# Moving a float32 decoder trunk's up-projections and mixer outputs to tokens on the partitions, with block transposes on VectorE and small transfers inside SBUF

## The chip, the cores and the metric

The kernel runs on one core of a Trainium2 chip. A core has a matrix engine (TensorE; PE in the profile, PEld for its weight loads), a vector engine (VectorE, DVE), a scalar engine (ScalarE, ACT), a general engine (GpSimd, POOL) and a queue engine (SyncE, SP). Each runs its own instructions in order and waits on semaphores for the others. Transfers are issued by SP, ACT or POOL and carried out by 16 DMA engines. SBUF is the on-chip memory of 128 partitions, PSUM the accumulators that TensorE writes. The metric is device time in microseconds (us) of one launch.

## The reference, cut to what matters

A residual stream `x` of 256 tokens by 2048 features goes through two layers, all in float32.

```python
h = rms_norm(x, mix_norm[l])
h = mixer_ab(h, ...)              # layer 0: gMLP (8 heads) beside HGRN2 (8 heads), then @ ab_w_out
h = mixer_c(h, ...)               # layer 1: forgetting attention, 16 heads, then @ c_w_out
x = x + h
h = rms_norm(x, ffn_norm[l])
z = h @ w_up                      # 2048 -> 2 * 5632
z = conv_w[0]*z[t-2] + conv_w[1]*z[t-1] + conv_w[2]*z[t] + conv_b    # per feature, along the tokens
a, b = split(z, 2)
x = x + (silu(a) * b) @ w_down    # 5632 -> 2048
```

The convolution runs along the tokens, so it wants a feature's tokens side by side in one partition.

## The kernel before, in words

**Products.** Every float32 operand of a large product is held as two rounded parts, high and low, and a product is three: high by high, low by high, high by low. `weights` (lines 130 to 142) loads a chunk of weights on SP, ScalarE makes the high part `wh` (line 139), VectorE the low part `wl` (line 141). `split` (199 to 206) does the same for activations; a tile of 512 columns holds 256 tokens of high part and then 256 of low part. A block below means 128 inputs by 128 outputs of a weight, over all 256 tokens.

There are two forms of a product. In `project` (144 to 161) the weights are the operand that TensorE holds and the activations stream past: per block one matmul of 512 columns with `wh` (line 155) and one of 256 columns with `wl` (line 158), and the output has features on the partitions. In `project_tok` (163 to 184) and in `down` (line 727 to 729) 128 tokens of activations are held and 512 output features stream past: three matmuls of 512 columns for each half of the tokens and each 128 inputs, and the output has tokens on the partitions. Four blocks then take six matmuls.

**Stages.** `mixer_ab` uses `project_tok` for v and i, `project` for f, q, g and u, and `project` for the output `w_abo`: 16 outputs of 16 blocks, each added to the stream `xT` by `add_x` (263) and handed to the next norm by `feed`, which splits it and adds its square to a running sum. `ffn` then runs `up` and `down`. `up` makes 11 hidden tiles at a time: `conv` (658) calls `project_norm`, that is a product in the first form, `fold` (ScalarE copies one half out of PSUM, VectorE adds the other), a multiplication by the norm's `R`, and the convolution (667 to 669) on ScalarE and VectorE; then silu, product and split. `down` accumulates each group of 11 in the token form into `y`; at the last group `turn` (688) transposes `y` on TensorE (line 692, 64 transposes in the program), except for the last quarter of the outputs, which uses `project` and `add_x`. `mixer_c` has q, k and v in token form, the gate in `project`, and its output `w_co` in `project` as `w_abo`. The number of blocks in the first form is 2816 in the two up-projections, 256 in each mixer output, 88 in `down` and 784 elsewhere: 4200.

**What sets the order.** The program is traced in Python and a scheduler orders each engine's instructions by when they could start, taking the traced order first among those that could. Work that may lie beside products is written as generators in `queue`; `tick`, called at each chunk of weights, advances at most `depth` of them by a step. `weights` draws from a pool `wp` with 4 buffers of `w` and 3 each of `wh` and `wl`; in the MLPs every other chunk uses a second pool (`deep`) with 4 and 2. PSUM has four banks for products (`pm`). At the start 15 matmuls on ones (WARM) run before the first product; the table FETCH sets when pieces of `x` are loaded, most of them on SP.

Of the kernel before, what the change touches and what calls it, by code (L numbers as in the profile page):

```python
# [14 lines left out]
P = 128  # L15
S = 256
# [6 lines left out]
GRP = 11  # L23
EPS = 1e-6
WARM = 15
FETCH = {0: (0,), 1: (1, 2, 8), 2: (4, 6), 3: (12,)}
# [19 lines left out]
def tile_trunk(ctx: ExitStack, tc: tile.TileContext, x, pp_d, cst_d, mlev_d, msk_d,  # L46
# [24 lines left out]
    pp = cp.tile([P, NPP], F32, tag="pp", name="pp")  # L71
    cst = cp.tile([P, NK], F32, tag="cst", name="cst")
    ones = cp.tile([P, P], F32, tag="ones", name="ones")
    one1 = cp.tile([P, 1], F32, tag="one1", name="one1")

    nc.sync.dma_start(pp[:, 0:C_FFN], pp_d[:, 0:C_FFN])
# [23 lines left out]
    def back(ap):  # L100
        return view(ap, P - 1, (-1, P))

# [27 lines left out]
    def weights(src, n, rows=None):  # L130
        deep["turn"] += 1
        if deep["pool"] is not None and deep["turn"] > 6 and deep["turn"] % 2:
            pool, nw, ns = deep["pool"], 4, 2
        else:
            pool, nw, ns = wp, 4, 3
        w = pool.tile([P, n], F32, tag="w", name=nm("w"), bufs=nw)
        nc.sync.dma_start(w if rows is None else w.rearrange("p (m c) -> p m c", m=rows), src)
        wh = pool.tile([P, n], F32R, tag="wh", name=nm("wh"), bufs=ns)
        SC.activation(wh, w, AF.Copy)  # L139
        wl = pool.tile([P, n], F32R, tag="wl", name=nm("wl"), bufs=ns)  # L140
        V.tensor_tensor(wl, w, wh.bitcast(F32), ALU.subtract)  # L141
        return wh, wl

    def project(wsrc, acts, chunks=(8, 8), k0=0, run=2):
        ps = pm.tile([P, 512], F32, tag="pm", name=nm("pm"))
        nk = sum(chunks)
        done = 0
        for c in chunks:
            lo = (k0 + done) * P
            tick()  # L150
            wh, wl = weights(wsrc[:, lo:lo + c * P], c * P)
            for k1 in range(0, c, run):
                ks = range(k1, min(k1 + run, c))
                for k in ks:
                    PE.matmul(ps, wh[:, k * P:(k + 1) * P], acts[done + k],  # L155
                              start=done + k == 0, stop=False, skip_group_check=True)
                for k in ks:
                    PE.matmul(ps[:, S:2 * S], wl[:, k * P:(k + 1) * P], acts[done + k][:, 0:S],  # L158
                              start=False, stop=done + k == nk - 1, skip_group_check=True)
            done += c  # L160
        return ps

    def project_tok(wsrc, norm, feed=False):
        ps = [pm.tile([P, 512], F32, tag="pm", name=nm("pm")) for _ in range(2)]
        k = 0
        for c in ((1, 1, 1, 1) + (2,) * 6 if feed else (2,) * 8):
            if feed:
                for c0 in FETCH.get(k, ()):
                    t, c0, n = fetch[c0]
                    (SC if c0 >= 8 else nc.sync).dma_start(t, x[:, c0:c0 + n, :])  # L170
                for i in range(c):
                    norm.feed_split(k + i)
            tick()
            wh, wl = weights(wsrc[:, k * 512:(k + c) * 512], c * 512)
# [9 lines left out]
        return ps  # L184

# [13 lines left out]
    def split(dst, src, gain=None):  # L199
        if gain is None:  # L200
            SC.activation(dst[:, 0:S], src, AF.Copy)
            V.tensor_tensor(dst[:, S:2 * S], src, dst[:, 0:S].bitcast(F32), ALU.subtract)
        else:
            SC.activation(dst[:, 0:S], src, AF.Copy, scale=gain)
# [3 lines left out]
    def rsq(dst, src, n):  # L208
        tag = "sq" if dst.shape[-1] == S else f"rm{len(dst.shape)}{dst.shape[-1]}"
        m = tp.tile(list(dst.shape), F32, tag=tag, name=nm("rm"))  # L210
        t = tp.tile(list(dst.shape), F32, tag=tag, name=nm("rt"))
# [11 lines left out]
    class Norm:  # L223
        def __init__(self, col):
            self.col = col
            self.a = [None] * KT
            self.acc = cp.tile([P, S], F32, tag="acc", name=nm("acc"), bufs=2)
            self.n = 0

        def feed_split(self, k):  # L230
            a = apool.tile([P, 512], F32R, tag="a", name=nm("a"), bufs=KT)
            split(a, xT[k], pp[:, self.col + k:self.col + k + 1])
            self.a[k] = a
# [13 lines left out]

        def finish(self, tok=False):
# [6 lines left out]
            p2 = bank()  # L255
            for T in range(2):
                PE.matmul(p2[:, 2 * T:2 * T + 2], self.acc[:, T * P:(T + 1) * P], ones[:, 0:2],
                          start=True, stop=True)
            Rt = cp.tile([P, 2], F32, tag="Rt", name=nm("Rt"), bufs=2)
            rsq(Rt, p2[:, 0:4].rearrange("p (t two) -> p t two", two=2)[:, :, 0], D)  # L260
            return R, Rt

    def add_x(m, ps):
# [3 lines left out]
        V.tensor_tensor(xT[m], xT[m], t, ALU.add)  # L267


    def mixer_ab(norm):  # L270
# [90 lines left out]
        ge = hp.tile([P, 3 * NH], F32, tag="ge", name="ge")  # L361
# [32 lines left out]
        def hgrn(h):  # L394
# [15 lines left out]
            for li in reversed(range(NL)):  # L410
# [8 lines left out]
                if li:  # L419
                    V.tensor_tensor(odd, odd, view(tot, m, (-m, 2), (2, m // 2), (0, n)), ALU.mult)  # L420
                    nt = hp.tile([P, m], F32, tag=f"tot{n}", name=nm("tot"), bufs=1)
# [34 lines left out]
            so = hp.tile([P, 2], F32, tag="so", name=nm("so"), bufs=2)  # L456
# [33 lines left out]
        def gated(b):  # L490
# [3 lines left out]
            split(yB[8 + b], lf[b])  # L494
            yield

        def spatial(b, z):
# [3 lines left out]
            split(yB[b], z)  # L501
# [20 lines left out]
        nxt = Norm(C_FFN)  # L522
        ks = [yB[8 + h] for h in range(NH)] + [yB[h] for h in range(NH)]
        for m in range(KT):
            add_x(m, project(w_abo[m], ks, run=2))
            nxt.feed(m)
# [4 lines left out]
    def mixer_c(norm):  # L531
# [4 lines left out]
        R, Rt = norm.finish(tok=True)  # L536
# [4 lines left out]
        gq = hp.tile([P, 1], F32, tag="gq", name="gq")  # L541
# [23 lines left out]
        def attend(h, q, k, v):  # L565
# [20 lines left out]
            mxs = hp.tile([P, 2], F32, tag="mxs", name=nm("mxs"), bufs=2)  # L586
            sms = hp.tile([P, 2], F32, tag="sms", name=nm("sms"), bufs=2)
# [22 lines left out]
        for g in range(CH // 4):  # L610
            qkv = []
            ss = hp.tile([P, 2, 2, 4], F32, tag="ss", name=nm("ss"), bufs=2)
            for j in range(3):
                ps = project_tok(w_cqkv[j * (CH // 4) + g], norm)
# [15 lines left out]
        for h in range(CH):  # L630
# [5 lines left out]
            for b, z in todo:  # L636
# [3 lines left out]
                split(yB[b], z)  # L640
            todo = []
        nxt = Norm(C_FFN + KT)
        for m in range(KT):
            add_x(m, project(w_co[m], yB, run=2))
            nxt.feed(m)
# [4 lines left out]
    def ffn(l, norm, last):  # L650
# [4 lines left out]
        R = norm.finish()  # L655
        nxt = None if last else Norm(C_MIX + KT)

        def conv(j):
            z = project_norm(w_up[l, j], A, R, run=2)

            def w(i):
# [4 lines left out]
            c = hp.tile([P, S], F32, tag="conv", name=nm("conv"), bufs=4)  # L666
# [5 lines left out]
        def up(g):  # L672
            hid = []
            for i in range(GRP):
                j = g * GRP + i
                a = conv(j)
                b = conv(HT + j)
                act(a, a, AF.Silu)
                V.tensor_tensor(a, a, b, ALU.mult)
                t = hp.tile([P, 512], F32R, tag="hid", name=nm("hid"), bufs=2 * GRP)  # L680
                split(t, a)
                hid.append(t)
            return hid
# [4 lines left out]
        def turn(m0):  # L688
            for m in range(m0, m0 + 4, 2):
                tps = bank()  # L690
                for i in range(4):
                    PE.transpose(tps[:, i * P:(i + 1) * P],  # L692
                                 y[:, i % 2, (m + i // 2) * P:(m + i // 2 + 1) * P], ident)
                for i in range(2):
                    V.tensor_tensor(xT[m + i], xT[m + i], tps[:, i * S:(i + 1) * S], ALU.add)
# [7 lines left out]
        def down(g, hid):  # L703
            final = g == HT // GRP - 1
            late = []
            for q in range(4):
                if final and q == 3:
                    for m in range(4 * q, KT):
                        ps = project(w_dn[l, m], hid, chunks=(6, 5), k0=g * GRP, run=2)
                        if late:  # L710
                            late.pop()()
                            turn(4 * q)
                        add_x(m, ps)
                        finish_x(m)
                    return
                ps = [pm.tile([P, 512], F32, tag="pm", name=nm("pm")) for _ in range(2)]
                for k in range(0, GRP, 2):
                    c = min(2, GRP - k)
                    lo = (g * GRP + k) * P
                    wh, wl = weights(w_dn[l, 4 * q:4 * q + 4, :, lo:lo + c * P]  # L720
                                     .rearrange("m p c -> p m c"), 4 * c * P, 4)
                    for T in range(2):
                        for i in range(c):
                            a = hid[k + i]
                            ah, al = a[:, T * P:(T + 1) * P], a[:, S + T * P:S + (T + 1) * P]
                            h, lo_ = (view(t, i * P, (c * P, 4), (1, P)) for t in (wh, wl))
                            PE.matmul(ps[T], ah, h, start=k + i == 0, stop=False)  # L727
                            PE.matmul(ps[T], ah, lo_, start=False, stop=False)  # L728
                            PE.matmul(ps[T], al, h, start=False, stop=k + i == GRP - 1)  # L729
                    if k == 4 and late:  # L730
                        late.pop()()
                for T in range(2):
                    d = y[:, T, q * 512:(q + 1) * 512]
                    if g == 0:
# [3 lines left out]
                if final:  # L738
                    def done(m0=4 * q):
                        turn(m0)  # L740
                        for m in range(m0, m0 + 4):
                            finish_x(m)
                    late.append(done)

        hids = [up(0)]
        for g in range(HT // GRP):
            if g + 1 < HT // GRP:
                hids.append(up(g + 1))
            down(g, hids[g])
# [88 lines left out]
```

## Time and profile before

Three runs took 2359.57, 2360.89 and 2361.82 us. The profiled execution took 2359.05 us, 1.85 us more than its span; the median is 1.84 us above it.

| | us | share of the span | instructions |
|---|---|---|---|
| span of the profiled execution | 2357.2 | | 33532 |
| PE | 2348.7 | 100% | 12528 |
| PEld | 2011.1 | 85% | 12528 |
| DVE | 1689.0 | 72% | 2760 |
| ACT | 1286.3 | 55% | 2085 |
| POOL | 0.2 | 0% | 4 |
| 16 DMA engines, SP's queue | | 55.3% | 193424 packets, 434.20 MB |

The granted TensorE clock was 1.000 throughout. A busy share is time in which the engine had an instruction in flight; matmuls overlap each other, so the rate of PE is read from the distance of their starts. In a group's line, "a | b, c | d" stands for shapes and count, busy us and mean ns of one, and idle us of the engine before them with what ended it. In the timeline a row is one or several instructions of a line: start, length, engine, line, operation, operands.

### The profile page before, as it was taken

Reading aid. Unit: us, or ns where it says so; the run is one execution under the profiler, and the core shown is the slowest. Engines: PE = TensorE matmul, PEld = TensorE weight load, DVE = VectorE, ACT = ScalarE, POOL = GpSimd, SP = SyncE. Lnnn points to the kernel's source line nnn. Section 1 sums busy time; section 2 is a strip of 40 time slices with the busy share of each in tenths; the row PEclk is TensorE's granted clock in tenths of the full one; section 3 lists DMA queues with packets and bytes.
Section 4 is the critical chain, followed back from the end, with each engine's and each line's share of the span. In section 5 each row is a group of like instructions: output and inputs, shape, how many; then the busy total and the mean of one; then the engine's idle time right before and its main releaser. Section 6 shows DMA issues by size and latency. Waiting matters only on the chain.

```text
span 2357.2 us, 33532 instructions
## 1 busy us (share of the span) xinstructions
PE 2348.7 (100%) x12528; PEld 2011.1 (85%) x12528; DVE 1689.0 (72%) x2760; ACT 1286.3 (55%) x2085; POOL 0.2 (0%) x4
## 2 busy tenths in 40 slices
PE   9999999999999999999999999999999999999999
PEld 7888888888888888888888888888888888888887
DVE  7777877878847757866766666777878757758755
ACT  7655665655545545544555455556555545545533
POOL 0000000000000000000000000000000000000000
PEclk9999999999999999999999999999999999999999
DMA  7544455655555565555655554556555565565563
GB/s 269 179 166 150 150 197 206 222 188 188 179 196 196 184 192 197 184 181 164 202 171 180 171 161 169 188 188 239 190 190 189 179 203 190 179 202 191 178 193 117
DMA packets 194740, 439.56 MB, mean 186 GB/s; under 512 B 14208, under 2 KB 108688, under 8 KB 194448
## 3 DMA queue, kind: packets, MB, share of 16 engines
q1 hardware_dynamic: 193424, 434.20, 55.3%
q10 hardware_dynamic: 1152, 3.21, 0.4%
q8 instruction: 98, 1.61, 0.3%
q14 instruction: 66, 0.54, 0.1%
HBM read 435.24 MB, written 2.11 MB: 186 GB/s over the span
## 4 chain that ended last, share of the span: by engine, by line
PE 99%; DMA 0%; ACT 0%; DVE 0%; SPq 0%; issue 0%; ACTq 0%
PE pm L155 42%; PE pm L158 21%; PE pm L728 6%; PE pm L727 6%; PE pm L729 6%; PE pm L181 5%; PE pm L182 5%; PE pm L180 5%; PE px L432 1%; DMA w<-in_w_v 0%; PE px L606 0%; PE px L692 0%; PE px L570 0%; PE px L577 0%; PE px L601 0%; PE px L402 0%
## 5 line engine op out<-in xcount | busy, mean ns | idle before, releaser
L141 DVE TENSOR_TENSOR wl<-w,wh 128x1024 fp32r<-128x1024 f32 (+1 forms) x840 | 1004.3, 1196 | 556.2 <-ACT wh L139 553.9
L139 ACT ACTIVATE wh<-w 128x1024 fp32r<-128x1024 f32 (+1 forms) x840 | 871.1, 1038 | 962.2 <-PE pm L155 473.1
L155 PE MATMUL pm<-a,wh 128*128 128x512 f32 x3600 | 1135.3, 396 | 0.0
L158 PEld LDWEIGHTS pm<-a,wl 128*128 128x128 f32 x3600 | 676.1, 188 | 158.9
L158 PE MATMUL pm<-a,wl 128*128 128x256 f32 x3600 | 708.7, 278 | 0.0
L155 PEld LDWEIGHTS pm<-a,wh 128*128 128x128 f32 x3600 | 549.6, 189 | 1.5 <-DVE a L205 0.8
L727 PE MATMUL pm<-wh,hid 128*128 128x512 f32 x660 | 257.1, 390 | 0.0
L728 PE MATMUL pm<-wl,hid 128*128 128x512 f32 x660 | 256.8, 389 | 0.0
L729 PE MATMUL pm<-wh,hid 128*128 128x512 f32 x660 | 256.8, 389 | 0.0
L180 PE MATMUL pm<-wh,a 128*128 128x512 f32 x512 | 203.1, 398 | 2.6 <-ACT wh L139 2.6
L181 PE MATMUL pm<-wl,a 128*128 128x512 f32 x512 | 200.8, 392 | 0.6 <-DVE wl L141 0.6
L182 PE MATMUL pm<-wh,a 128*128 128x512 f32 x512 | 200.2, 391 | 0.0
L729 PEld LDWEIGHTS pm<-wh,hid 128*128 128x128 f32 x660 | 123.9, 188 | 25.7
L727 PEld LDWEIGHTS pm<-wh,hid 128*128 128x128 f32 x660 | 123.9, 188 | 25.5
L728 PEld LDWEIGHTS pm<-wl,hid 128*128 128x128 f32 x660 | 123.9, 188 | 25.3
L180 PEld LDWEIGHTS pm<-wh,a 128*128 128x128 f32 x512 | 96.2, 188 | 22.4 <-ACT wh L139 3.7
L181 PEld LDWEIGHTS pm<-wl,a 128*128 128x128 f32 x512 | 96.2, 188 | 21.3 <-DVE wl L141 2.2
L182 PEld LDWEIGHTS pm<-wh,a 128*128 128x128 f32 x512 | 96.1, 188 | 19.8
L667 ACT ACTIVATE conv<-ev,pp 128x256 f32<-128x256 f32 x176 | 102.9, 585 | 5.5 <-DVE ev L196 5.5
L189 DVE TENSOR_TENSOR ev<-pm,ev 128x256 f32<-128x256 f32 x225 | 93.9, 417 | 1.1 <-ACT ev L188 1.0
L669 DVE SCALAR_TENSOR_TENSOR conv<-ev,pp,conv 128x254 f32<-128x254 f32 x176 | 85.0, 483 | 6.2
L668 DVE SCALAR_TENSOR_TENSOR conv<-ev,pp,conv 128x255 f32<-128x255 f32 x176 | 84.1, 478 | 4.4 <-ACT conv L667 4.4
(185 smaller groups left out, 1644.3 us busy)
## 6 DMA issues: line engine op xcount, KB each, us to landing
w<-in_w_up SPq DMA_DIRECT2D x352, 512.0 KB, 4.2
w<-in_w_dn SPq DMA_DIRECT2D x150, 512.0 KB, 3.6
w<-in_w_cqkv SPq DMA_DIRECT2D x96, 512.0 KB, 3.5
w<-in_w_abo SPq DMA_DIRECT2D x32, 512.0 KB, 3.6
w<-in_w_cg SPq DMA_DIRECT2D x32, 512.0 KB, 3.6
w<-in_w_co SPq DMA_DIRECT2D x32, 512.0 KB, 3.6
w<-in_w_f SPq DMA_DIRECT2D x16, 512.0 KB, 3.7
w<-in_w_q SPq DMA_DIRECT2D x16, 512.0 KB, 3.6
```

Of the source, the lines that this page charges most:

```text
L139: SC.activation(wh, w, AF.Copy)
L141: V.tensor_tensor(wl, w, wh.bitcast(F32), ALU.subtract)
L155: PE.matmul(ps, wh[:, k * P:(k + 1) * P], acts[done + k], start=done + k == 0, stop=False, skip_group_check=True)
L158: PE.matmul(ps[:, S:2 * S], wl[:, k * P:(k + 1) * P], acts[done + k][:, 0:S], start=False, stop=done + k == nk - 1, skip_group_check=True)
L180: PE.matmul(ps[T], ah, h, start=k + i == 0, stop=False)
L181: PE.matmul(ps[T], ah, l, start=False, stop=False)
L182: PE.matmul(ps[T], al, h, start=False, stop=k + i == KT - 1)
L189: V.tensor_tensor(t, ps[:, 0:S], t, ALU.add)
L667: SC.activation(c, z, AF.Identity, bias=pp[:, cb:cb + 1], scale=w(2))
L727: PE.matmul(ps[T], ah, h, start=k + i == 0, stop=False)
L728: PE.matmul(ps[T], ah, lo_, start=False, stop=False)
L729: PE.matmul(ps[T], al, h, start=False, stop=k + i == GRP - 1)
```

## The change

The up-projections of both MLPs and the two mixer outputs go to the token form: `project_four` takes four columns of blocks at once, in chunks of two inputs, and each of the two halves of the tokens gets one PSUM bank. A half now holds every other token: `split(..., turn=True)` reads the 256 tokens with step 2. What follows still wants features on the partitions, so `transposed` turns the result back. VectorE transposes the 32 x 32 squares of a 128 x 512 tile where they stand (two instructions), and 16 transfers inside SBUF, each 32 partitions by 4 runs of 64 numbers (32 KB, 128 pieces of 256 bytes), carry the squares to their places; 8 are issued by SP and 8 by POOL. The consumers are generators that begin LAG = 4 ticks later. Multiplication by the norm's factor moves into the copy out of PSUM, with the factor per token (`Rt`, from `finish_tok`), and `R` is no longer made for the MLPs.

The TensorE transposes of `y` go; `add_y` uses `transposed`. Only the last quarter of the last output stays in `project`, its last column with 256-column matmuls alone (`narrow`). `down` takes 12, 12, 12 and 8 hidden tiles (STEPS). The second weights pool has 2 buffers of `w` in place of 4. `mixer_c` starts its first product before the norm's factors are made. At the start, the first weights are issued first on SP and the first five pieces of `x` on ACT's queue, WARM is 11, and VectorE makes the first high part. Small tiles are padded to 16 numbers (LANE). The diff, cut to what is spoken of:

```diff
-GRP = 11
+STEPS = ((3, 1), (3, 1), (3, 2), (2, 0))
+BLK = 32
+LAG = 4
-WARM = 15
-FETCH = {0: (0,), 1: (1, 2, 8), 2: (4, 6), 3: (12,)}
+WARM = 11
+FETCH = {4: (8,), 8: (12,)}
+LANE = 16
...
+    first = wp.tile([P, 512], F32, tag="w", name=nm("w"), bufs=4)
+    nc.sync.dma_start(first, w_v[0, :, 0:512])
+    for t, c0, n in xload[:5]:
+        SC.dma_start(t, x[:, c0:c0 + n, :])
     nc.sync.dma_start(pp[:, 0:C_FFN], pp_d[:, 0:C_FFN])
...
+    def turned(ap):
+        return view(ap, 0, (1, 2), (2, P))
...
-            pool, nw, ns = deep["pool"], 4, 2
+            pool, nw, ns = deep["pool"], 2, 2
...
+    def project_four(w4, acts, n, k0=0):
+        ps = [pm.tile([P, 512], F32, tag="pm", name=nm("pm")) for _ in range(2)]
+        for k in range(0, n, 2):
+            tick()
+            lo = (k0 + k) * P
+            wh, wl = weights(w4[:, :, lo:lo + 2 * P].rearrange("m p c -> p m c"), 1024, 4)
+            for T in range(2):
+                for i in range(2):
+                    a = acts[k + i]
+                    ah, al = a[:, T * P:(T + 1) * P], a[:, S + T * P:S + (T + 1) * P]
+                    h, l = (view(t, i * P, (2 * P, 4), (1, P)) for t in (wh, wl))
+                    PE.matmul(ps[T], ah, h, start=k + i == 0, stop=False)
+                    PE.matmul(ps[T], ah, l, start=False, stop=False)
+                    PE.matmul(ps[T], al, h, start=False, stop=k + i == n - 1)
+        return ps
+
+    def transposed(src, tmp, dst):
+        for T in range(2):
+            V.transpose(tmp.rearrange("p (b m i t) -> p b m i t", b=4, m=4, t=2)[:, :, :, :, T],
+                        src(T).rearrange("p (m b j) -> p b m j", m=4, b=4))
+        n = 2 * BLK
+        for a in range(4):
+            for b in range(4):
+                (nc.sync, nc.gpsimd)[(a + b) % 2].dma_start(dst[BLK * b:BLK * (b + 1), :, a * n:(a + 1) * n],
+                                  tmp[BLK * a:BLK * (a + 1), b * 4 * n:(b + 1) * 4 * n]
+                                  .rearrange("p (m r) -> p m r", m=4))
...
+        def finish_tok(self):
+            p2 = bank()
+            for T in range(2):
+                lhs = self.acc[:, T * P:(T + 1) * P] if not self.turn else view(self.acc, T, (2, P))
+                PE.matmul(p2[:, 2 * T:2 * T + 2], lhs, ones[:, 0:2], start=True, stop=True)
+            Rt = cp.tile([P, LANE], F32, tag="Rt", name=nm("Rt"), bufs=2)[:, 0:2]
+            yield
+            rsq(Rt, p2[:, 0:4].rearrange("p (t two) -> p t two", two=2)[:, :, 0], D)
+            self.Rt = Rt
...
+    def add_four(q, ps, z, tmp, dst, nxt):
+        for T in range(2):
+            SC.activation(z[:, T], ps[T], AF.Copy)
+        transposed(lambda T: z[:, T], tmp, dst)
+
+        def rest():
+            for _ in range(LAG - (q == 3)):
+                yield
+            for i in range(4):
+                m = 4 * q + i
+                V.tensor_tensor(xT[m], xT[m], dst[:, i], ALU.add)
+                nxt.feed(m)
+                if q < 3 or i % 2:
+                    yield
+            if q == 3:
+                yield
+                yield from nxt.finish_tok()
+
+        queue.append(rest())
...
-        for m in range(KT):
-            add_x(m, project(w_abo[m], ks, run=2))
-            nxt.feed(m)
+        for q in range(4):
+            ps = project_four(w_abo[4 * q:4 * q + 4], ks, KT)
...
+            add_four(q, ps, z, tmp, dst, nxt)
...
-        def conv(j):
-            z = project_norm(w_up[l, j], A, R, run=2)
+        def four(j0):
+            ps = project_four(w_up[l, j0:j0 + 4], A, KT)
+            Rt = norm.Rt
+            tmp, zt = room()
+            z = [hp.tile([P, 512], F32, tag="z", name=nm("z"), bufs=3) for _ in range(2)]
+            for T in range(2):
+                SC.activation(z[T], ps[T], AF.Copy, scale=Rt[:, T:T + 1])
+            transposed(lambda T: z[T], tmp, zt)
+            return zt
...
+        def up(j0):
+            za = four(j0)
+            ca = []
+
+            def gate():
+                for _ in range(LAG):
+                    yield
+                for i in range(4):
+                    a = conv(za[:, i], j0 + i, 0)
+                    act(a, a, AF.Silu)
+                    ca.append(a)
+                    yield
+
+            queue.append(gate())
+            zb = four(HT + j0)
...
-        def turn(m0):
...
+        def add_y(q, finish):
+            tmp, zt = room()
+            transposed(lambda T: y[:, T, q * 512:(q + 1) * 512], tmp, zt)
...
+                    for m in range(4 * q, KT):
+                        end = m == KT - 1
+                        ps = project(w_dn[l, m], hid, chunks=(n,), k0=k0, run=2, narrow=end)
...
+                        V.tensor_tensor(x2, x2, view(ps, 0, (1, P), (P, 2)), ALU.add)
                         finish_x(m)
```

`room` gives one buffer `tmp` and two of `zt`. A second generator, `fill`, does the other half's convolution, the product with the gate and the split, four tiles in four ticks.

232 lines of the change are left out of this document (136 added, 96 removed).

## The prediction

> **What bounds the kernel now.** I read the page's engine totals first, then the chain that ended last, then the waits, then PE's timeline inside single stages.
>
> ```profile
> span 2357.2 us, 33532 instructions
> PE 2348.7 (100%) x12528; PEld 2011.1 (85%) x12528; DVE 1689.0 (72%) x2760; ACT 1286.3 (55%) x2085; POOL 0.2 (0%) x4
> PE 99%; DMA 0%; ACT 0%; DVE 0%; SPq 0%; issue 0%; ACTq 0%
> ACT wh L139 <- PE pm L155: 473.1, 392, 2.9
> q1 hardware_dynamic: 193424, 434.20, 55.3%
> ```
>
> PE is the bound everywhere: 99% of the chain is its own work, and the fourth line shows that ScalarE, which makes the weights' high parts, waits for PE to give buffers back, not the other way round. So a change gains only by giving PE less to do, and loses when PE is kept waiting. PE's two forms of product, from its timeline:
>
> ```profile
> 440.29 0.63 PE L155 MATMUL pm<-a,wh 128*128 128x512 f32 x2
> 462.59 0.63 PE L155 MATMUL pm<-a,wh 128*128 128x512 f32 x2
> ...
> 329.93 0.63 PE L155 MATMUL pm<-yb,wh 128*128 128x512 f32 x2
> 352.55 0.63 PE L155 MATMUL pm<-yb,wh 128*128 128x512 f32 x2
> ...
> 1059.75 0.39 PE L727 MATMUL pm<-wh,hid 128*128 128x512 f32 x1
> 1072.67 0.39 PE L727 MATMUL pm<-wh,hid 128*128 128x512 f32 x1
> ```
>
> Between the first two rows (up-projection) the pattern "two L155, two L158" runs 32 times, 64 blocks in 22.30 us: 0.348 us a block. Between the next two (`w_abo`) 64 blocks take 22.62 us: 0.353. Between the last two (token form) lie 57 matmuls in 12.92 us: 0.2267 each, and at 1.5 matmuls a block 0.340. Both forms stream 768 columns a block; the token form has 1.5 instructions where the other has 2, and that is the difference. Idle PE is found only at the ends:
>
> ```profile
> 7.50 0.73 PE L180 MATMUL pm<-wh,a 128*128 128x512 f32 x2 [1.36 <-ACT wh L139]
> 17.05 0.50 PE L181 MATMUL pm<-wl,a 128*128 128x512 f32 x1 [0.40 <-DVE wl L141]
> 2353.37 0.38 ACT L265 ACTIVATE ev<-pm 128x256 f32<-128x256 f32 x1 [3.50 <-PE pm L158]
> 2354.24 0.42 DVE L267 TENSOR_TENSOR x<-x,ev 128x256 f32<-128x256 f32 x1
> ```
>
> The first product starts at 7.50, and by 17.05 the timeline has 26 matmuls, worth 5.9 us, in 9.55. At the end a copy, two additions and the last transfer follow the last matmul.
>
> **The change part by part**, against the span 2357.2 (the run is 1.85 us longer, the median of the runs 1.84 more).
>
> *Blocks that change form.* 2816 in the up-projections by 0.0084 is 23.7; 256 in `w_abo` by 0.0134 is 3.4; 256 in `w_co` and 56 of `down` (88 less the 32 left in layer 1) by 0.0084 is 2.6. Together -29.7 us. The operand shapes of `project_four` are those of line 727, so I use that row as it is. The Trainium skill, "TensorE: Matmul & The Clock Gate", Back-to-back issue gap, has N/2.4 + 2.5 ns for a single matmul; by it a block would take 0.325 us in one form and 0.324 in the other, and this term would be about -4 us, the sum about 2351. The rows differ (0.2327 and 0.1157 against 0.2267), and the rows decide.
>
> *TensorE transposes.* The chain has them at 0.87 us for eight, so 64 go for -7.0 us. `R` of the two MLPs goes and `finish_tok` comes: L250 at 0.53 a pair against four tiny matmuls, -0.3 us.
>
> *Start.* The first weights no longer stand behind two other transfers on SP. Bounds: 0, and -5.4 (3.65 us lost between 7.50 and 17.05, and 1.8 before it if the product starts when x lands, about 5.7). The transfers still share the same 16 engines, so I take the middle, -2.5.
>
> *VectorE and ScalarE* are off the chain. Per four columns (64 blocks) VectorE has now 8 low parts of 1.224, four `fold` of 0.417, four multiplications of 0.425, eight convolution steps of 0.48, and silu products and splits of 1.69: 18.7 us beside 22.3 of PE. It loses `fold` and multiplication (3.4) and gains two transposes of 128x512. The trace has no such instruction; its rows of that shape take 0.684 to 0.688 whatever they do, so 1.4 (ends 0.7 and 2.8, if twice as fast or half). It has then 16.7 beside 21.8. ScalarE has 13.8 before and after. Cost nothing, hidden by PE.
>
> *Transfers.* 44 fours in the up-projections, 8 in the mixer outputs, 8 in `add_y`: 60, of 16 transfers and 2048 pieces of 256 bytes. By the trace's packet records a piece of 1024 bytes takes 52 ns, of 512 28, of 272 20. At 20 ns a four takes 2.6 us of the 16 engines beside 21.8. The up-projection's window shows a share of 0.61; weights in 1024-byte pieces cost 4 x 52 where one of 4096 takes 191, and the share becomes about 0.80. Ends: 9 ns (a piece of 4 bytes) and 52: share 0.73 to 1.0. I take 20, by the row of 272. Hidden, but with less cover than before: see the rivals. SP's 8 issues of 0.328 (its rows) are 2.6 us in 21.8, and behind them wait the next weights; what hides that is 6 buffers of `w` (8 before), each worth 2.72 us of PE.
>
> *The chain from a four's last matmul to its turned tile.* ScalarE copies 2 x 0.69 (row L617), transposes 1.4, transfers, landing 1.8 (the row out<-x). SP's share takes 2.6. POOL issues nothing in the trace: ends 0.33 a transfer (SP's) and 1.5 (the longest SP issue, 1.535). Nothing makes it nearer to one, so I take the middle, 0.9: 7.2 for eight. The tile is there 11.8 us after the matmul (7.2 to 16.6). In the steady state the consumers stand four ticks later and the chain costs nothing. It shows where PE needs the result at once:
>
> - the three passages (mixer A/B to MLP, MLP to mixer C, mixer C to MLP). The last outputs give inputs 12 to 15, which the next product needs six chunks in, 16.3 us after the last matmul. They are ready at 11.8 + 0.42 + 0.50 + 0.48 = 13.2 for the first pair, plus whatever conversions of 1.06 and 1.22 stand before them. Ends 0 and 5 us each; I take 1.0 each, +3.0.
> - the tail. After the third quarter of the last output PE has 32 blocks, 11.2 us, then one addition and a transfer: 14.1. The third quarter needs 1.4 for sums, 1.4, 7.2, 1.8, four additions of 0.42 and a transfer of 1.8: 15.3. +1.2 (ends 0 and 6). The last column itself has one addition for a copy and two, -0.9.
>
> LANE has its part in the 0.353 of `w_abo`, if it has one; WARM and `early` I cost at nothing: PE has work there already.
>
> Sum: 2357.2 - 29.7 - 7.0 - 0.3 - 2.5 + 3.0 + 1.2 - 0.9 = 2321.0; with 1.85 a run of 2322.9, and with 1.84 a median of 2324.7. I say 2325.
>
> **The rivals.**
>
> *The turned tiles come late, and ScalarE stands (slower).* `gate` puts its first convolution on ScalarE ahead of the fifth chunk's high part of the next four. With five buffers of `wh`, ScalarE has made the fourth chunk's before the last four's final matmul, so an order as traced would hold it from there until the tile lands. PE has four chunks, 10.9 us; the convolution, high and low part need 2.9. So PE stops once the tile takes more than 8.0 us, and 11.8 us would cost 3.8 at each of 52 fours: 2325 + 198 = 2523. Against it: the order is not the traced one. In the traced order 17 weight transfers stand behind the first four out<-x on SP, and only 5 come after them in SP's timeline; so what is not ready is passed. If the scheduler expects the tile when it comes, the cushion is five chunks, 13.6 us, beyond that time. The kernel is slower than before once the mean loss passes 36/52 = 0.7 us a four; with 1 to 3 us it takes 2377 to 2481. The Trainium skill, "SBUF — State Buffer", SBUF: two separate sides, speaks for this rival: transfers issued by GpSimd wait for descriptors while VectorE runs certain one-input operations. By that rule little is lost here, as such operations are few in these stages; no run here shows it.
>
> *The DMA engines become the bound (slower).* Weights take 13.4 us of a four's 21.8 (4096 pieces of 52 ns on 16 engines). The small pieces fill the rest when one takes over 65 ns. Nothing in the trace goes that way (256 bytes lie between rows of 17 and 28), but no transfer of it goes inside SBUF. At 80 ns: +1.8 us in each of 52 fours, 2421.
>
> *The passages and the tail cost their upper ends, and small waits stay in the fours.* +12 for passages, +5 for the tail, up to 0.3 a four: 2325 + 17 to 32, that is 2342 to 2357.
>
> *The rate does not differ.* If the new products run at 0.348 a block, 26 of the 30 us go: 2351. Against it, row 727 with the same shapes.
>
> **How the numbers follow.** Forecast, 2312 to 2342: 0.58. Upper ends, 2342 to 2357: 0.15. No difference in rate: 0.02. Late tiles: 0.18, most of it between 2366 and 2450. DMA bound: 0.05. Something between: 0.02. The measurement can tell 0.2%, 4.7 us, so "same" is 2356.2 to 2365.6. Faster 0.74, same 0.04 (the top of the upper ends, the foot of the late tiles), slower 0.22. The range 2308 to 2385 leaves out 0.03 below and some 0.15 above.
>
> **What would show it.** In the changed profile: starts of the matmuls of `project_four` 0.227 apart; no PE line of transposes of `y`; PE's count at 12528 - 3384 x 0.5 and about 64 less; DVE's groups of `fold` and the multiplication gone, and transposes near 0.69; POOL's queue with 480 transfers, whose length is the number I know least; packets of 256 bytes near 20 ns. Wrong it is if PE waits for `wh` or `wl` in the middle of the MLPs, if ScalarE's waits end at DMA zt, or if the chain that ended last shows DVE, ACT or DMA beyond a few per cent.

## The result, and the profile after

The changed kernel takes 2357.35 us, the median of 20 runs (2356.36 to 2359.36), beside 2360.88 for the kernel before: a ratio of 0.9985, 95% interval 0.9978 to 0.9991. That is 3.5 us or 0.15% faster, where 36 had been forecast. One of the 20 runs of the kernel before took 3916 us and stands alone; the ratio leaves it out. The profiled execution took 2357.62 us, with a span of 2355.8.

From the page of the changed kernel: span, engine totals, the two DMA queues that carry the weights and the small transfers, and the engines of the chain that ended last.

```profile
span 2355.8 us, 31594 instructions
...
PE 2340.0 (99%) x10776; PEld 1931.0 (82%) x10776; DVE 1583.3 (67%) x2470; ACT 1291.8 (55%) x1955; POOL 260.1 (11%) x484
...
q1 hardware_dynamic: 415904, 449.96, 62.3%
q0 software_dynamic: 15360, 15.76, 3.1%
...
PE 95%; DMA 1%; DVE 1%; SPq 1%; issue 1%; ACT 0%; POOL 0%; DVEq 0%; ACTq 0%; POOLq 0%
```

PE has 1752 matmuls less and is still the bound: 95% of the chain, where it was 99%. So the work went as described, the chain has 4 to 5% of other things in it, and the 10776 matmuls that are left take nearly as long as the 12528 before. Two views say where the time is. The first is the busy time in two stretches in the middle of the MLPs, away from their ends (length, then busy us and count of PE, PEld, DVE, ACT and POOL, the granted clock, the DMA share and GB/s):

```profile
540.00:1020.00 480.00, 480.00 (x2086) 391.30 (x2085) 306.24 (x404) 261.25 (x342) 65.83 (x122) 1.00 0.70 208
1740.00:2220.00 480.00, 480.00 (x2086) 391.30 (x2085) 306.51 (x404) 260.79 (x342) 64.94 (x120) 1.00 0.69 207
```

PE never stops in these 960 us, at full clock, and all its rows are matmuls of 512 columns in the token form. But 2086 in 480 us is one in 0.2301, not in 0.2267. The second view is the timeline at the passage from mixer A/B to the MLP. Behind it stand the windows of this passage and of the one from mixer C to the MLP:

```profile
402.66 17.16 SPq L150 DMA_DIRECT2D w<-in_w_up  x11
...
406.48 1.09 DVE L359 TENSOR_TENSOR x<-x,stage 128x256 f32<-128x256 f32 x3
...
413.35 0.63 PE L326 MATMUL px<-ones,acc 128*128 128x2 f32 x4 [0.99 <-DVE acc L315]
414.41 1.06 ACT L153 ACTIVATE wh<-w 128x1024 fp32r<-128x1024 f32 x1 [0.95 <-DMA w<-in_w_up]
...
415.52 1.22 PE L229 MATMUL pm<-wh,a 128*128 128x512 f32 x2 [1.53 <-ACT wh L153]
...
417.79 0.63 PE L229 MATMUL pm<-wh,a 128*128 128x512 f32 x1
...
420.78 0.63 PE L231 MATMUL pm<-wh,a 128*128 128x512 f32 x1
```

```profile
411.00:433.00 22.00, 19.44 (x74) 14.91 (x73) 12.57 (x17) 11.24 (x16) 4.33 (x8) 0.84 0.71 222
1630.00:1655.00 25.00, 22.20 (x91) 17.40 (x90) 14.17 (x18) 13.42 (x18) 4.33 (x8) 0.93 0.70 218
```

PE stands for 2.5 us around 413 and 415, first 0.99 for the running sum that `finish_tok` reads, then 1.53 for a high part whose weights had not landed. From 414.70 on, that is within the second wait, the granted clock is half for 6.8 us: between 417.79 and 420.78 lie seven matmuls, 0.427 us each. The passage from mixer C to the MLP looks the same, with 2.8 us of standing in three pieces and 3.4 us of half clock.

The new work on the other engines is hidden in the middle of the MLPs. Two of its groups in the changed kernel (count, busy us and mean ns, then the idle time before them):

```profile
L237 DVE STREAM_TRANSPOSE tmp<-z 128x512 f32<-128x512 f32 x88 | 61.9, 707 | 26.8 <-ACT z L777 26.8
...
L242 POOL DMA_DIRECT2D zt<-tmp x416 | 225.1, 549 | 1237.3 <-DVE tmp L237 1150.5
```

A transpose takes 0.707 us and an issue on POOL 0.549; in the two stretches above none of it reaches PE, which is busy for all of 960 us.

### The profile page after: what moved, and what is told of

It reads as the page before. It is cut to its first block, busy times and chain, and to the rows that moved or that the text cites. A ratio compares the mean times of both kernels' runs of the same rounds, so it can differ in the third digit from the quotient of the medians.

```text
span 2355.8 us, 31594 instructions
## 1 busy us (share of the span) xinstructions
PE 2340.0 (99%) x10776; PEld 1931.0 (82%) x10776; DVE 1583.3 (67%) x2470; ACT 1291.8 (55%) x1955; POOL 260.1 (11%) x484
## 4 chain that ended last, share of the span: by engine, by line
PE 95%; DMA 1%; DVE 1%; SPq 1%; issue 1%; ACT 0%; POOL 0%; DVEq 0%; ACTq 0%; POOLq 0%
PE pm L230 22%; PE pm L231 22%; PE pm L229 22%; PE pm L176 8%; PE pm L213 5%; PE pm L214 5%; PE pm L212 5%; PE pm L179 4%; SPq L242 1%; PE px L532 1%; DMA w<-in_w_up 0%; DMA x<-in_x 0%; PE px L713 0%; ACT wh L153 0%; PE px L677 0%
## 5 line engine op out<-in xcount | busy, mean ns | idle before, releaser
L229 PE MATMUL pm<-wh,a 128*128 128x512 f32 x1408 | 553.4, 393 | 2.8 <-ACT wh L153 1.5
L230 PE MATMUL pm<-wl,a 128*128 128x512 f32 x1408 | 553.9, 393 | 0.6 <-DVE wl L155 0.5
L231 PE MATMUL pm<-wh,a 128*128 128x512 f32 x1408 | 554.2, 394 | 0.0
L242 POOL DMA_DIRECT2D zt<-tmp x416 | 225.1, 549 | 1237.3 <-DVE tmp L237 1150.5
L229 PEld LDWEIGHTS pm<-wh,a 128*128 128x128 f32 x1408 | 265.1, 188 | 62.8 <-ACT wh L153 3.0
L230 PEld LDWEIGHTS pm<-wl,a 128*128 128x128 f32 x1408 | 265.4, 188 | 62.2 <-DVE wl L155 1.7
L231 PEld LDWEIGHTS pm<-wh,a 128*128 128x128 f32 x1408 | 265.2, 188 | 59.8
L231 PE MATMUL pm<-wh,hid 128*128 128x512 f32 x688 | 270.0, 392 | 0.0
L229 PE MATMUL pm<-wh,hid 128*128 128x512 f32 x688 | 269.7, 392 | 0.0
L176 PE MATMUL pm<-a,wh 128*128 128x512 f32 x784 | 251.0, 400 | 0.0
L212 PE MATMUL pm<-wh,a 128*128 128x512 f32 x504 | 200.1, 398 | 0.3 <-ACT wh L153 0.3
L213 PE MATMUL pm<-wl,a 128*128 128x512 f32 x504 | 197.4, 392 | 2.2 <-DVE wl L155 2.2
L214 PE MATMUL pm<-wh,a 128*128 128x512 f32 x504 | 197.0, 391 | 0.0
L179 PEld LDWEIGHTS pm<-a,wl 128*128 128x128 f32 x784 | 147.3, 188 | 34.2
L179 PE MATMUL pm<-a,wl 128*128 128x256 f32 x784 | 155.1, 279 | 0.0
L176 PEld LDWEIGHTS pm<-a,wh 128*128 128x128 f32 x784 | 120.5, 189 | 0.4
```

The source lines that it names most:

```text
L176: PE.matmul(ps, wh[:, k * P:(k + 1) * P], acts[done + k], start=done + k == 0, stop=False, skip_group_check=True)
L213: PE.matmul(ps[T], ah, l, start=False, stop=False)
L214: PE.matmul(ps[T], al, h, start=False, stop=k + i == KT - 1)
L230: PE.matmul(ps[T], ah, l, start=False, stop=False)
L231: PE.matmul(ps[T], al, h, start=False, stop=k + i == n - 1)
L242: (nc.sync, nc.gpsimd)[(a + b) % 2].dma_start(dst[BLK * b:BLK * (b + 1), :, a * n:(a + 1) * n], tmp[BLK * a:BLK * (a + 1), b * 4 * n:(b + ...
```

## The experiments

Two losses were to be explained, and two theories stood for them. *Addresses*: the matmuls are slower where the two operands start at different places in SBUF. Addresses are told by what is left when they are divided by 256 bytes; operands that leave the same are called in step. In the program before, the allocation puts `w`, `wh`, `wl`, `a`, `hid`, `yc` and `y` all 128 bytes past a multiple of 256 (`ya` and `yb` 224). In the changed program the first set of weights and `a` start at multiples of 256, `hid`, `y`, `yc` and the second set of weights 128 past one, because the padded small tiles lie between them; `ya` and `yb` start at multiples of 256 there. The rival was that the transfers, or the form itself with its strided view of the weights, slow the matmuls. *Passages*: two waits, of the kind shown above, against the rival that the turned tiles of the last four come late. Ratios below are to the kernel before in the same set of runs (2362.19, 2361.39 and 2360.82 us in the three sets); these medians lie up to 1.4 us apart, and a difference between kernels of different sets is no better known.

**All operands at multiples of 256.**

```diff
         cols = dst.shape[-1] if dst.shape[-1] == S else LANE // math.prod(dst.shape[1:-1])
+        if len(dst.shape) == 2 and dst.shape[-1] == 2:
+            cols = 2 * LANE
```

> Theory (the new products lose the gain of their form to where their operands lie in SBUF): with the pool of small tiles 128 bytes longer, weights, a, hid, y and yc all start at a multiple of 256 bytes; starts of the MLPs' matmuls go from about 230 to 227 ns apart; 6624 matmuls by 3.5 ns is 23 us, less about 1.5 us because ya and yb now lie 128 bytes off: about 2336 (2332 to 2340). Rival (the rate is lost to the small transfers, to SBUF traffic or to the strided view of the weights, whatever the addresses): 2355 to 2359, starts still 230 apart.

Measured: 2335.56 us, ratio 0.9893 (0.9879 to 0.9906), some 22 us faster than the changed kernel by 128 bytes of unused memory. The same window as above, of this kernel:

```profile
540.00:1020.00 480.00, 480.00 (x2120) 397.57 (x2119) 311.76 (x409) 264.73 (x346) 70.49 (x131) 1.00 0.68 211
```

2120 in 480 us is one in 0.2264. The transfers, the form and the strided view are all still there; the rival falls.

**The padding undone.**

```diff
-LANE = 16
+LANE = 2
```

> The changed kernel with LANE = 2 in place of 16, so that one part of the change, the padding of small tiles, is undone. All weights, a, hid, y and yc then start 128 bytes past a multiple of 256, as before the change; only ya and yb (at 0) are off. Theory (the padding put the operands of every second weight buffer out of step): as the aligned kernel, 2335 to 2337. Rival (the padded kernel is slow for another reason, and 128 bytes more happened to help): 2350 to 2358.

Measured: 2335.9 us, ratio 0.9893 (0.9879 to 0.9906), and 2120 matmuls in the same 480 us. So it is LANE, one constant of the change, that put the operands out of step. In this kernel the common start is 128 past a multiple of 256, in the aligned one it is 0, and both are fast: it is not one place that is good.

**The kernel before, put out of step.**

```diff
-        m = tp.tile(list(dst.shape), F32, tag=tag, name=nm("rm"))
-        t = tp.tile(list(dst.shape), F32, tag=tag, name=nm("rt"))
+        wide = list(dst.shape[:-1]) + [24 if list(dst.shape) == [P, 2] else dst.shape[-1]]
+        m = tp.tile(wide, F32, tag=tag, name=nm("rm"))[..., 0:dst.shape[-1]]
+        t = tp.tile(wide, F32, tag=tag, name=nm("rt"))[..., 0:dst.shape[-1]]
```

> The kernel before with nothing changed but 64 bytes more in each of two pairs of unused columns, so that the MLP's pool (hid, the second set of weights) moves by 128 bytes against a and the first set of weights. Theory (addresses set the rate): every second weight buffer is now off against its partner, in up and in down; about 1000 of down's matmuls by 3 to 7 ns and half of 2816 up blocks by 5 ns: slower by 6 to 14 us, 2367 to 2375. Rival (the rate belongs to what is new in the changed kernel, not to addresses): 2359 to 2363.

Measured: 2372.18 us, ratio 1.0046 (1.0033 to 1.0060), 10 us slower. The kernel before has no small transfers and no strided weights, and pays as well. In `down`, the distance of starts goes from 226.8 ns to 232.5 with the first set of weights and to 228.0 with the second; in the up-projections the 256-column matmuls go from 115.2 to 118.9 ns where the second set is used, and the 512-column ones stay at 233.

**Another distance.**

```diff
+        if len(dst.shape) == 2 and dst.shape[-1] == 2:
+            cols = 3 * LANE // 2
```

> The changed kernel with its pool of small tiles 64 bytes longer: the second set of weights, hid, y and yc start 192 bytes past a multiple of 256, a and the first set at 0 (so partners are 64 or 192 off where they were 128 off). If any distance that isn't a multiple of 256 costs the same: 2353 to 2359. If the cost falls with the distance (in the runs so far, on 256 columns: 32 off 3 ns, 128 off 4.4, 96 off 6): 2343 to 2352. If multiples of 64 are free: 2335 to 2337.

Measured: 2361.43 us, ratio 1.0004 (0.9995 to 1.0013). That is 2 us above the first case's upper end. `ya` and `yb`, now 64 off too, are worth 2.3 us of it (384 matmuls by 6 ns). In sum the distances of 64 and 192 cost as much as those of 128; pair by pair they do not, as the table shows.

These runs together give the following table ("distance 64" is the kernel just named). It takes every start of a token-form matmul from the trace and the operands' addresses from the compiled program, where the matmuls stand in the same order; distances of starts outside 180 to 260 ns (stalls, half clock) are left out. The streamed operand is the weights, the held one the activations; both are given modulo 256.

| streamed at | held at | mean distance of starts, ns (count, kernel) |
|---|---|---|
| 0 | 0 | 226.8 (8086, aligned), 227.6 (4004, changed), 228.0 (1080, before out of step) |
| 128 | 128 | 226.8 (8068, LANE = 2), 227.1 (3413, before), 227.9 (1032, changed) |
| 0 | 128 | 232.6 (1416, changed), 232.4 (384, aligned: `ya`, `yb`) |
| 128 | 0 | 232.6 (2017, changed), 232.5 (896, before out of step) |
| 192 | 0 | 233.3 (2017, distance 64) |
| 0 | 64 | 233.3 (384, distance 64: `ya`, `yb`) |
| 0 | 192 | 229.9 (1416, distance 64) |
| 192 | 192 | 230.6 (1032, distance 64) |

It is fast where both start at a multiple of 256, or both 128 past one. The last row shows that a common start is not enough, and the two rows above it, of the same distance to one side and to the other, that the distance alone does not set the cost. What in the chip does this the runs do not show. The Trainium skill, "TensorE: Matmul & The Clock Gate", Step-by-step: what each phase is for, gives TensorE two independent read ports into SBUF, one for the streamed and one for the held operand; by that alone one would not expect one operand's place to matter to the other's, and the first four rows say that it does.

**The passages.**

```diff
-        if deep["pool"] is not None and deep["turn"] > 6 and deep["turn"] % 2:
+        if deep["pool"] is not None and deep["turn"] > 10 and deep["turn"] % 2:
...
             if q == 3:
-                yield
+                for _ in range(4):
+                    yield
                 yield from nxt.finish_tok()
...
+            while norm.Rt is None:
+                tick()
             Rt = norm.Rt
```

The same three yields are added in `add_y`.

> The changed kernel, with the second set of weight buffers first used at turn 11 in place of 7, and the matmul of finish_tok put behind the last chunk of the next product. Theory (at the passages PE stands behind those two waits, and then runs at half clock): the idle 3.5 us at 412 and 4 us at 1631 and the half clock behind them go; 8 to 10 us faster than the changed kernel: 2348 (2346 to 2350). Rival (the turned tiles of the last four set the passage, whatever waits ahead of them): less than 2 us, 2355 to 2358, and the clock still falls to half.

Measured: 2346.05 us, ratio 0.9934 (0.9921 to 0.9948), 11 us faster than the changed kernel. That is a little more than expected. Matched start by start (each matmul of one kernel beside the one of the same number in the other), 6.0 us come from the passage at 412 and 5.2 from that at 1631; all else together differs by 0.2. PE's window from 300 to 540 goes from 237.44 busy at a clock of 0.99 to:

```profile
300.00:540.00 240.00, 240.00 (x1066) 197.63 (x1065) 167.84 (x240) 141.15 (x201) 43.41 (x80) 1.00 0.72 221
```

The turned tiles come no earlier here (the first addition of `stage` starts at 406.52, in the changed kernel at 406.48), so they were not what PE waited for.

**Both edits**, with one more pad that brings `ya` and `yb` to a multiple of 256:

```diff
+            cols = 2 * LANE
...
-        ss = hp.tile([P, 4 * NH], F32, tag="ss", name="ss")
+        ss = hp.tile([P, 8 * NH], F32, tag="ss", name="ss")[:, 0:4 * NH]
...
+        if deep["pool"] is not None and deep["turn"] > 10 and deep["turn"] % 2:
```

> The edits of the aligned kernel and of the passages kernel together, and ya and yb brought to a multiple of 256 bytes too. Theory: the two gains add: 2357 - 23 - 9 is about 2325 (2320 to 2330). Rival (both are the same microseconds, or neither is real): no better than the better one of the two alone, 2336 or more.

Measured: 2322.01 us (2321.28 to 2322.46), ratio 0.9834 (0.9820 to 0.9847). The gains add. This is the fastest kernel here, 1.7% under the one before; its page:

```profile
span 2320.3 us, 31588 instructions
...
PE 2310.4 (100%) x10776; PEld 1928.4 (83%) x10776; DVE 1583.0 (68%) x2470; ACT 1290.2 (56%) x1955; POOL 260.1 (11%) x484
...
PE 98%; DMA 1%; DVE 1%; SPq 0%; ACT 0%; issue 0%; DVEq 0%; POOLq 0%
```

**Which of the two waits.** From the kernel of both edits, first the second set of weights is used from turn 7 on again:

> The kernel of both edits (2322 us) with the second set of weight buffers again first used at turn 7. Theory (the larger wait at the passages is the 7th chunk's weight transfer, which starts only when the mixer's memory is free, and the idle 3 us brings the half clock): 5 to 9 us slower, 2327 to 2331. Rival (finish_tok's matmul was the larger, and behind it the transfer is in time): under 1.5 us, 2321 to 2323.5.

Measured: 2334.17 us, ratio 0.9884 (0.9871 to 0.9898), 12 us slower, more than expected: 6.4 at the first passage and 5.1 at the second. Then the second set starts at turn 11 as in the kernel of both edits, and `finish_tok` goes back ahead of the 7th chunk:

> The kernel of both edits (2322 us) with finish_tok's matmul back ahead of the 7th chunk. Theory (PE's queue stands at it for about 1 to 1.5 us at two passages, too short for the half clock): 1.5 to 4 us slower, 2323.5 to 2326. Rival (it is the whole of the passages' loss): 9 to 13 us slower, 2331 to 2335.

Measured: 2323.25 us, ratio 0.9838 (0.9825 to 0.9851), 1.2 us slower, a little less than expected and no more than the runs can tell apart, since the two intervals overlap. PE around the first passage in the kernel of both edits, with the early turn, and with the early `finish_tok`, one view each:

```profile
402.00:422.00 20.00, 20.00 (x92) 16.59 (x91) 15.35 (x24) 12.83 (x20) 0.00 (x0) 1.00 0.82 272
```

```profile
402.00:422.00 20.00, 17.21 (x66) 13.39 (x65) 13.15 (x23) 11.39 (x18) 0.13 (x1) 0.85 0.89 288
```

```profile
402.00:422.00 20.00, 19.93 (x90) 16.25 (x89) 15.66 (x27) 15.01 (x23) 0.26 (x1) 1.00 0.83 272
```

The counts of matmuls tell it: 92, 66, 90. With the early turn PE is idle for 2.8 us and then at half clock; with the early `finish_tok` it stands for 0.07 and the clock stays at 1.00. So nearly the whole loss is the weights of the 7th chunk. It is the first chunk of the second pool, whose memory is the mixer's, so its transfer can be issued only after the last addition that reads `stage`. In the changed kernel SP's queue stands from 407.37 and issues it at 410.19, right behind that addition (409.70 to 410.12), and ScalarE can begin on it at 414.41. The tiles are not what is late: the first of the four additions starts at 406.48, and the last stands behind VectorE's other work. At turn 11 there is nothing left to wait for.

**The issues of the small transfers.** From the kernel of both edits, all 16 of a four on one queue, first SP, then POOL:

```diff
-                (nc.sync, nc.gpsimd)[(a + b) % 2].dma_start(...)
+                nc.sync.dma_start(...)
```

> The kernel of both edits with all 16 small transfers of a four issued by SP, none by POOL: 16 times 0.60, or 9.7 us of SP in a four of 21.8, in place of 4.8; the tile lands some 5 us later. Theory (the cover of four ticks and five buffers holds these 5 us too; only the tail shows them): 2322 + 4.5, 2324 to 2330. Rival (late tiles hold ScalarE, as the slower rival of the prediction has it): 1 us or more in each of 52 fours, 2360 and above.

Measured: 2515.99 us, ratio 1.0657 (1.0643 to 1.0672). The theory falls: the cover does not hold. But the time is not yet the rival's, since two things changed, the tile's landing and the weights' place behind 16 issues.

```diff
-                (nc.sync, nc.gpsimd)[(a + b) % 2].dma_start(...)
+                nc.gpsimd.dma_start(...)
```

> The kernel of both edits with all 16 small transfers of a four issued by POOL (16 times 0.55 is 8.8 us in a row), none by SP. The tile lands some 4 us later than in the kernel of both edits, about as late as in the SP-only kernel, but SP's queue holds only weights. Theory (the SP-only kernel lost its time to weights that stood behind 11 us of issues, not to the late tile): 2322 + 3 to 6 for the tail, 2323 to 2328. Rival (the late tile holds ScalarE, whoever issues): 2400 and above.

Measured: 2357.16 us, ratio 0.9986 (0.9976 to 0.9995). The middle of the MLP, with all issues on SP, and then with all on POOL:

```profile
540.00:1020.00 480.00, 458.23 (x1966) 372.71 (x1964) 285.09 (x372) 239.80 (x317) 0.00 (x0) 0.98 0.62 194
```

```profile
540.00:1020.00 480.00, 480.00 (x2118) 397.25 (x2117) 310.18 (x410) 262.36 (x346) 142.19 (x263) 1.00 0.68 212
```

With POOL's 16 issues in a row the tile is late too: the first step of the convolution starts 14.7 us after the transposes, where it is 7.7 in the kernel of both edits and 13.6 with SP alone (medians over the 44 fours of the up-projections). And PE has all of 480 us: inside the MLPs a tile that late costs nothing. With SP it loses 22 of 480. The timeline of the SP-only kernel shows the way:

```profile
604.13 11.25 SPq L242 DMA_DIRECT2D zt<-tmp  x16
...
615.48 7.55 SPq L150 DMA_DIRECT2D w<-in_w_dn  x5
...
619.74 1.04 ACT L153 ACTIVATE wh<-w 128x1024 fp32r<-128x1024 f32 x1
...
620.83 0.73 PE L229 MATMUL pm<-wh,hid 128*128 128x512 f32 x2 [2.61 <-ACT wh L153]
```

SP issues no weights for 11.25 us here; 16 issues of 0.617 on average are 9.9. Issue to landing takes 4.6 us for these weights (the page's median) and the two conversions 2.3; together 18.2, or 16.8 on average, against six buffers of `w` worth 16.3 us of PE. With 8 issues on SP (5.1 us) the same sum is 12.0 and fits. The POOL-only kernel's 35 us above the kernel of both edits, far more than expected, lie at the ends: matched start by start, 19.6 up to the last matmul, nearly all at the passages (1.4 at the first, 13 on the way to mixer C, 4 at the next), and 16 behind it. On the way to mixer C and behind the last matmul two sets of 16 issues follow each other because both write one `tmp`. There the result is needed at once, and a late tile does cost.

## Why the prediction was right or wrong

The direction was right and the time lies inside the range, but the size was off by 32 us of 36. That it lies inside the range is no merit of the argument: the range reached to 2385 for the sake of late tiles, which did not come, and the time stands where the prediction gave 0.04, between 2356.2 and 2365.6. By the prediction's own terms, on spans (2357.2 before, 2321.0 forecast, 2355.8 measured):

- *Blocks that change form, -29.7.* This is the term that failed, in the step "The operand shapes of `project_four` are those of line 727, so I use that row as it is." Shapes were the same, addresses were not: line 727's operands all lay 128 past a multiple of 256, and the change moved half of the new ones. Over the stretches of the MLPs and `w_co` the passages kernel, whose operands lie as the changed kernel's, takes 24.0 us more than the kernel of both edits for the same matmuls, so the term was worth about -6. With operands in step it is what was forecast: 576 matmuls of an up-projection take 130.56 us, 0.2267 each, where the changed kernel takes 132.65. `w_abo`, whose operands happen to be in step in the changed kernel, went from 90.66 to 87.07 us, -3.59 for a forecast of -3.4. The part of LANE in its 0.353, left open, is seen too: `ya` and `yb` lay 96 bytes off, and their 256-column matmuls took 121.2 ns where others took 115.4. That the gain of the form comes from the number of instructions, as the prediction says, no run shows: at starts that are in step a matmul of 512 columns takes 226.8 ns in the token form and 233 in the other.
- *The rival "the rate does not differ", 2351, given 0.02.* Its time is close, its reason is not the one found: the forms do differ, by the rows, once the operands are in step. The rule that stood beside it (the Trainium skill, "TensorE: Matmul & The Clock Gate", Back-to-back issue gap) gives 215.8 ns for 512 columns; in no kernel here does the mean come under 226.
- *The rival of the upper ends, 2342 to 2357, given 0.15*, is the nearest in time. It was right on the passages (about 10 us above what was forecast, 12 allowed) and wrong on the rest: its small waits in the fours are not there, PE being busy for all of the 960 us shown.
- *Passages, +3.0.* This is the second step that failed. Measured are 6.0 and 5.2 us at the two entries to an MLP, and 1.6 of idle time on the way to mixer C, 1.2 of it in one wait for a low part; 13 in all, inside the ends of 0 to 15. The cause was not named. The prediction looked for conversions ahead of the last inputs; it was the first use of the second weights pool, and of its price at the first entry more than half is the half clock that goes with 2.5 us of standing.
- *Start, -2.5*: the product that follows the first one starts 2.35 us earlier (53.43 for 55.77). *Tail, +1.2 and -0.9*: the end lies 5.6 us behind the last matmul's start, 4.2 before, so +1.4 in all for +0.3. By the terms that the prediction names, 11.2, 0.42 and 1.8, PE's side of the tail is 13.4 and not 14.1, so its +1.2 would have been +1.9.
- *TensorE transposes, -7.0*: PE's count fell by 1752, as 3384 halves and 60 more. Their time was not measured by itself.
- *What was hidden stays hidden.* SP's issue of a small transfer takes 0.60 us and not the 0.328 assumed; POOL's 0.549 (0.9 assumed, ends 0.33 and 1.5); a transpose 0.707 (0.69). By the packet records a piece of 256 bytes on SP's queue takes 19.6 ns (20 assumed); POOL's queue moves the same bytes in pieces of 2048 at 141 ns. For a four in the middle of the first MLP the first step of the convolution starts 9.3 us after the copy of its last half could begin (667.50 to 676.78; 11.8 assumed for the tile). The DMA share there is 0.70, so the rival of the DMA engines did not happen either.
- *The rival of late tiles, 0.18*, did not happen. ScalarE does stand for the tile (40.3 us in 24 waits), and PE does not notice. The POOL-only kernel answers the rival's sum, by which PE stops once the tile takes more than 8.0 us: there the issues (8.65) and the landing (4.2) alone take 12.9, and PE does not stop in the MLPs. But the sentence beside it, that the next weights wait behind SP's issues and six buffers hide them, was the closer danger: at 16 issues it breaks, and the kernel takes 2516. The Trainium skill, "SBUF — State Buffer", SBUF: two separate sides, has GpSimd's transfers wait for their descriptors while VectorE runs certain operations; here POOL's land in 2.4 us and SP's in 2.5 (medians), so in the medians no such wait shows.

The kernel of both edits has a span of 2320.3, beside the 2321.0 forecast: with the two faults taken away, the sum of the terms comes out. That it does so to 0.7 us is partly luck: the passages in it are 1.4 us cheaper and the tail 1.1 us dearer than was said, and the two cancel.

```profile
2340.09 1.31 DVE L237 STREAM_TRANSPOSE tmp<-y 128x512 f32<-128x512 f32 x2
...
2341.43 5.11 SPq L242 DMA_DIRECT2D zt<-tmp  x8
...
2349.44 1.09 DVE L834 TENSOR_TENSOR x<-x,zt 128x256 f32<-128x256 f32 x3 [0.37 <-DMA out<-x]
```

This is the changed kernel's tail: SP's eight issues take 5.11 us where 2.6 were assumed for SP and 7.2 for POOL, and the four additions come after the last columns' own.

## What to carry to other kernels

Before a matmul's row is used for a new product, compare the start addresses of its operands as well as their shapes: a constant that pads small tiles moved every later buffer, and with it 1% of the time. A buffer that takes over another stage's memory should not be the one that is needed first at the passage, and a stall of some microseconds on TensorE there is to be priced with the half clock that came with it, here 3.4 us beside 2.5 of standing and 1.7 beside 2.8. Count the issues on the queue that also carries the weights, with the issue time of the transfer in question.

## What the runs showed of the hardware

- The rate of TensorE depends on where its operands start in SBUF: in the token form 226.8 to 228.0 ns for 512 columns when both start at a multiple of 256 bytes or both 128 past one, 232.4 to 232.6 when one is at the one and one at the other, 230 to 233 when one or both are at 64 or 192. For 256 columns it is 115.4 against 118 to 121.
- With 2.5 us of standing (two pieces within 3.2 us) the granted clock was 0.5 for 6.8 us, and with 2.8 us (three pieces within 4.2) for 3.4; no single piece is longer than 1.53 us. With 0.07 us at a passage, or 1.2 us on the way to mixer C, it stayed at 1.0. At the half clock a 512-column matmul took 0.427 us. The Trainium skill, "TensorE: Matmul & The Clock Gate", Wait — 56ns, not 53.3ns?, has 426.7 ns for it, and the trace agrees.
- An issue on SP takes 0.60 us for a transfer of 128 pieces of 256 bytes (median; in the row of 16 shown 0.70 each), and 0.37 for a chunk of weights in the MLPs; on POOL the same transfer takes 0.549.
